# Differential attention in a decoder layer: q, k and v projected in six groups of 512 columns, kept in memory as rows, and read back by half heads

## The chip, the core and the metric

The kernel runs on one core of a Trainium2 chip. TensorE (PE) multiplies; PEld is its load of the stationary operand, which overlaps PE. VectorE (DVE), ScalarE (ACT) and GpSimd (POOL) work beside it, and SyncE (SP) issues nearly all DMAs, one after the other. Each of these engines runs its own instructions in order. The metric is the device time of one execution in microseconds, as the median of several runs.

## The reference, cut to what matters

One layer with three parallel branches, a gated merge and an MLP, on 1024 positions of width 1024, in float32. Only branch B, the differential attention, is touched:

```
proj = rms_norm(x, norm_mix_g) @ w_in              # dq, dk, dv are 1024 columns each
q = rms_norm(dq per head and half, q_g); k = rms_norm(dk per head and half, k_g)
s = q @ k^T * scale, causal                         # 8 heads x 2 halves of width 64
a = softmax(s of half 0) - lam * softmax(s of half 1)
o = rms_norm(a @ v, subln_g) * (1 - lam_init)       # v: 128 columns a head
```

The gates of the merge, `h @ w_gate`, are 3072 further columns of a projection of the same h. Nothing in the attention needs them; the kernel uses them as filler.

## The kernel before, in words

All products are made of float32r pieces: `split` turns a float32 tile into a high part (an ACT cast) and a low part (a DVE subtraction), and `mm3` issues three matmuls for each pair of split operands. The normed input lies in SBUF for the whole stage as `hT` (8 blocks of 128 features, high and low, 1024 positions).

Branch B is `branch_d`. It walks through 64 steps `s`: 8 heads times 8 blocks of 128 query positions. A step computes the scores of both halves (`scores`: PE, then a mask and maximum on DVE, an exponential on ACT), combines them (`combine`, DVE), transposes the result one step later (`turn`: PE into a bank of PSUM, split by ACT and DVE), and two steps later multiplies it with v (`values`). Between these pieces `fill(n)` advances a generator by n units; a unit is the `mm3` of one of the 8 feature blocks, three matmuls. Instructions of PE are pinned: they stay in the order in which the code is written. The other engines' orders are set by a scheduler when the kernel is built, and each engine then keeps to its order.

The generator is `d_gemm`, and gate projections (`gate_steps`) when it has run out. Before the change it works by half heads: for each of 8 heads it loads and splits 8 weight tiles of 384 columns (128 of q, of k and of v), and for each of the head's 8 blocks of positions it fills one PSUM bank in 8 units of 3 matmuls with 384 moving columns. ACT then copies q and k out of the bank (`draw`), squares them and casts v; DVE subtracts v's low part from the bank (`dv`) and sums the squares. After four blocks, half a head is ready: `rsqrt_mean` on POOL, then three late pieces at fixed units of the next half: `q_` (four transposes on PE into `pr`, a split into `dsg`, four DMAs), `s_` (k times its reciprocal norm: four DVE products on `draw`) and `k_` (four transposes, a split, four DMAs to `dk`). The banks of the projection are two, `mm0` and `mm1`, in turn; `pr` takes the one that is not being filled, and the projection's next tile takes the bank of `pr`. So k_'s split has to be done when the next tile begins.

`branch_d` starts with `fill(60)`, then 8 units a step. Of the 12 groups of gate columns (32 units each), the first 6 run before the branch, the last two of these alone on PE, and the rest within it and after it.

Of the kernel before, what the change touches and what calls it, by code (L numbers as in the profile page):

```python
# [10 lines left out]
F32 = mybir.dt.float32  # L11
# [9 lines left out]
NT = 8  # L21
# [50 lines left out]
class Layer:  # L72
# [11 lines left out]
    nmm, kmm = 0, 2  # L84
# [362 lines left out]
    def gate_steps(self, runs):  # L447
# [4 lines left out]
        for run in runs:  # L452
            for r in range(run):
# [3 lines left out]
                for q in range(4):  # L457
# [401 lines left out]
    def d_gemm(self, pool, kv, done):  # L859

        nc = self.nc
        V = nc.vector
        late = []

        def prep(raws, rr, vh):

            qT = pool.tile([P, 2, 512], F32R, tag="dq", name=self.name("dq"))
            kk = pool.tile([P, 2, 2, 512], F32R, tag="dk", name=self.name("dk"))
            rows = [slice(0, 64), slice(64, 128)]

            def turned(j):
                pt = self.other_tile()
                for i in range(4):
                    self.transpose(pt[:, i * P : (i + 1) * P], raws[i][:, j * P : (j + 1) * P])
                return pt, pool.tile([P, 2, 512], F32R, tag="dsg", name=self.name("dsg"))

            def q_():
                pt, sg = turned(0)
                self.split(sg[:, 0], sg[:, 1], pt, self.gd)
                for c in range(2):  # L880
                    for h in range(2):
                        nc.sync.dma_start(f32(qT[rows[h], c]), f32(sg[rows[c], h]))

            def s_():
                for i in range(4):
                    k_ = raws[i][:, P : 2 * P].rearrange("p (c d) -> p c d", c=2)
                    self.pin(V.tensor_mul(k_, k_, rr[:, i, 2:4].unsqueeze(2).broadcast_to([P, 2, 64])))

            def k_():
                pt, sg = turned(1)  # L890
# [4 lines left out]
                kv.append((qT, kk[:, 0], kk[:, 1], vh, rr))  # L895

            return [(4, q_), (5, s_), (13, k_)]
# [3 lines left out]
        def wload(hd, k):  # L901
            r = self.rp.tile([P, 768], F32, tag="raw", name=self.name("raw"))
            nc.sync.dma_start(r.rearrange("p (k n) -> p k n", k=2), self.a["wd"][hd][:, k : k + 2, :])
            raw[hd, k] = r[:, 0:384]
            raw[hd, k + 1] = r[:, 384:768]

        def wsplit(hd, k, w):
            t = self.wp.tile([P, 2, 384], F32R, tag="w", name=self.name("w"))
            self.split(t[:, 0], t[:, 1], raw.pop((hd, k)))
            w[k] = (t[:, 0], t[:, 1])  # L910
            if k == 1:
                wload(hd, 6)

        nw = {}
        for j in range(16):
            hd, hf = divmod(j, 2)
            if j == 0:
                wload(0, 0)
                wload(0, 2)
                wload(0, 4)  # L920
                for k in range(NK):
                    wsplit(0, k, nw)
            if hf == 0:
                w, nw = nw, {}
            rr = pool.tile([P, 4, 4], F32, tag="drr", name=self.name("drr"))
            vh, raws = [], []
            for i in range(4):
                t = hf * 4 + i
                ps = self.mm_tile(384)
                for k in range(NK):  # L930
                    s = slice(t * P, (t + 1) * P)
                    self.mm3(ps, (self.hT[:, k, 0, s], self.hT[:, k, 1, s]), w[k], k == 0, k == NK - 1)
                    if hf and hd < 7:
                        if i == 1 and k == 0:
                            wload(hd + 1, 0)
                            wload(hd + 1, 2)
# [834 lines left out]
```

## Time and profile before

| | |
|---|---|
| median of 3 runs | 2215.06 us (2214.48 to 2216.39) |
| the profiled execution | 2213.57 us, its span 2211.8 us |
| busy in the span | PE 98%, PEld 84%, DVE 62%, ACT 44%, POOL 24% |
| granted clock of TensorE | 0.995 over the span, 1.00 in every stretch read here |
| DMA | 273 MB, mean 123 GB/s |

Branch B with its projections takes from about 620 us to 1150 us. PE busy is the share of time in which at least one matmul was under way; since a matmul's record is longer than the distance to the next one's start, rates are read from starts, not from durations. Where 28 matmuls are shown merged in one row, the next row's start tells when the last of them had gone in.

### The profile page before, as it was taken

Reading aid. Unit: us, or ns where it says so; the run is one execution under the profiler, and the core shown is the slowest. Engines: PE = TensorE matmul, PEld = TensorE weight load, DVE = VectorE, ACT = ScalarE, POOL = GpSimd, SP = SyncE. Lnnn points to the kernel's source line nnn. Section 1 sums busy time; section 2 is a strip of 40 time slices with the busy share of each in tenths; the row PEclk is TensorE's granted clock in tenths of the full one; section 3 lists DMA queues with packets and bytes.
Section 4 is the critical chain, followed back from the end, with each engine's and each line's share of the span. In section 5 each row is a group of like instructions: output and inputs, shape, how many; then the busy total and the mean of one; then the engine's idle time right before and its main releaser. Section 6 shows DMA issues by size and latency. Waiting matters only on the chain.

```text
span 2211.8 us, 30588 instructions
## 1 busy us (share of the span) xinstructions
PE 2163.4 (98%) x11097; PEld 1860.7 (84%) x11097; DVE 1361.4 (62%) x2598; ACT 980.7 (44%) x1962; POOL 527.8 (24%) x696
## 2 busy tenths in 40 slices
PE   7999999999999999999999999999999999899999
PEld 5878888898899999999888888877787888688887
DVE  6643575565237777777641232544688877767779
ACT  6543355454336666666542120223444444543332
POOL 2100000000011111111000003202557655565553
PEclk9999999999999999999999999999999999999999
DMA  7023122121333333333343443436435444854444
GB/s 250 29 81 115 50 91 76 44 82 39 107 109 86 93 84 84 88 92 86 101 148 114 134 142 126 138 110 205 147 115 198 159 147 147 318 196 146 145 145 170
DMA packets 127948, 273.06 MB, mean 123 GB/s; under 512 B 12945, under 2 KB 21430, under 8 KB 125750
## 3 DMA queue, kind: packets, MB, share of 16 engines
q1 hardware_dynamic: 125494, 258.53, 37.2%
q10 hardware_dynamic: 2304, 12.58, 1.4%
q8 instruction: 87, 1.43, 0.3%
q14 instruction: 63, 0.52, 0.1%
HBM read 178.76 MB, written 67.14 MB: 111 GB/s over the span
## 4 chain that ended last, share of the span: by engine, by line
PE 77%; DVE 9%; DMA 6%; ACT 4%; issue 2%; POOL 2%; SPq 0%; DVEq 0%; ACTq 0%; POOLq 0%
PE mm L91 46%; PE p L91 20%; PE sc L91 6%; PE tp L94 2%; PE po L91 2%; DVE acc L67 1%; DMA kraw<-y 1%; DMA xr<-h_d 1%; DVE wo L67 1%; DMA y<-yd 1%; DVE u L67 1%; DVE w L112 1%; DMA wraw<-in_wup 0%; DVE xts L67 0%; DVE c L67 0%
## 5 line engine op out<-in xcount | busy, mean ns | idle before, releaser
L91 PE MATMUL mm<-w,hT 128*128 128x384 f32 (+3 forms) x2496 | 473.4, 332 | 8.3 <-DVE dsg L112 5.4
L91 PE MATMUL mm<-hT,w 128*128 128x512 f32 x1920 | 465.7, 395 | 0.0
L91 PEld LDWEIGHTS mm<-hT,w 128*128 128x128 f32 x1920 | 353.5, 188 | 74.2
L91 PEld LDWEIGHTS mm<-w,hT 128*128 128x128 f32 x2496 | 389.2, 190 | 22.2 <-DVE dsg L112 7.6
L91 PE MATMUL p<-xd,wo 128*128 128x512 f32 x1344 | 310.0, 393 | 5.7 <-DVE c L67 2.2
L91 PE MATMUL p<-xo,wo 128*128 128x512 f32 x1344 | 308.2, 390 | 5.7 <-DVE st L1418 2.6
L91 PEld LDWEIGHTS p<-xd,wo 128*128 128x128 f32 x1344 | 253.8, 189 | 61.7 <-DVE c L67 3.3
L91 PEld LDWEIGHTS p<-xo,wo 128*128 128x128 f32 x1344 | 251.0, 188 | 61.5 <-DVE u L67 3.7
L91 PE MATMUL mm<-kt,w 128*128 128x512 f32 x1152 | 262.2, 389 | 1.9 <-ACT w L111 1.1
L112 DVE TENSOR_TENSOR w<-raw,w 128x256 fp32r<-128x256 f32 (+3 forms) x304 | 173.0, 590 | 137.9 <-ACT w L111 136.8
L91 PEld LDWEIGHTS mm<-kt,w 128*128 128x128 f32 x1152 | 216.0, 188 | 47.9 <-ACT w L111 1.5
L111 ACT CAST w<-raw 128x256 fp32r<-128x256 f32 (+3 forms) x304 | 154.3, 530 | 178.9 <-PE mm L91 114.5
L104 ACT CAST wo<-wraw 128x896 fp32r<-128x896 f32 x122 | 115.0, 945 | 208.9 <-PE p L91 115.2
L67 DVE TENSOR_TENSOR wo<-wraw,wo 128x896 fp32r<-128x896 f32 x122 | 143.7, 1195 | 59.4 <-ACT wo L104 59.4
L1145 POOL TENSOR_TENSOR wraw<-wraw 128x128 f32<-128x128 f32 x128 | 97.3, 760 | 245.8 <-DMA wraw<-in_wdown 108.1
L1007 ACT ACTIVATE dpe<-sc,dst,drr 128x256 f32<-128x256 f32 (+7 forms) x128 | 106.7, 834 | 99.7 <-DVE dst L1003 92.0
L999 DVE CUSTOM_DVE_ANT_0 sc<-sc,tmask 128x256 f32<-128x256 f32 (+7 forms) x128 | 97.0, 758 | 12.6 <-PE sc L91 12.5
L127 POOL TENSOR_SCALAR hss<-hss 128x4 f32<-128x4 f32 x8 | 3.3, 410 | 415.4 <-ACT mscr L752 272.9
L91 PE MATMUL sc<-dk,dq 128*128 128x512 f32 (+3 forms) x384 | 90.4, 343 | 0.0
L1148 POOL TENSOR_TENSOR wraw<-wraw 128x128 f32<-128x128 f32 x128 | 85.6, 669 | 10.0
L1146 POOL TENSOR_TENSOR wraw<-wraw 128x128 f32<-128x128 f32 x128 | 87.3, 682 | 0.0
L1147 POOL TENSOR_TENSOR wraw<-wraw 128x128 f32<-128x128 f32 x128 | 87.2, 682 | 0.0
(283 smaller groups left out, 2832.6 us busy)
## 6 DMA issues: line engine op xcount, KB each, us to landing
dk<-dsg SPq DMA_DIRECT2D x64, 256.0 KB, 4.4
wraw<-in_wup SPq DMA_DIRECT2D x64, 256.0 KB, 3.4
r_d<-xts SPq DMA_DIRECT2D x16, 1024.0 KB, 4.1
wraw<-in_wdown SPq DMA_DIRECT2D x64, 256.0 KB, 3.1
xd<-r_d SPq DMA_DIRECT2D x19, 768.0 KB, 7.4
xd<-r_d SPq DMA_DIRECT2D x14, 1024.0 KB, 6.8
raw<-in_wgate SPq DMA_DIRECT2D x48, 256.0 KB, 3.2
gates<-gt SPq DMA_DIRECT2D x48, 256.0 KB, 2.0
```

What stands on the lines that cost most here:

```text
L67: return self.tc.keep_in_program_order(f(*a, **k))
L91: self.pin(self.nc.tensor.matmul(out, l, r, start=start, stop=stop))
L94: self.pin(self.nc.tensor.transpose(out, x, self.ident))
L104: self.A.copy(hi, src)
L111: nc.scalar.copy(hi, src)
L112: nc.vector.tensor_sub(lo, src, f32(hi))
L999: V.tensor_tensor_reduce(out=sc[:, 0:n], in0=sc[:, 0:n], in1=self.tmask[:, D - n : D], scale=1.0, scalar=-3.0e38, op0=ALU.add, op1=ALU.max ...
L1007: nc.scalar.activation(pe[c][:, 0:n], sc[:, 0:n], AF.Exp, bias=t8[:, 2 + c : 3 + c], scale=rr[:, i, c : c + 1], accum_out=t8[:, 4 + c : 5 ...
L1145: G.tensor_add(r[:, 4], r[:, 0], r[:, 3])
L1146: G.tensor_sub(r[:, 5], r[:, 4], r[:, 1])
L1147: G.tensor_sub(r[:, 6], r[:, 1], r[:, 0])
L1148: G.tensor_sub(r[:, 7], r[:, 2], r[:, 5])
```

## The change

Projections are made in six groups of 512 columns instead of eight of 384 (the columns stay in the order of heads, so a head's 384 columns lie in one group or in two). Each finished tile of 128 positions and 512 columns is copied out of PSUM whole by ACT (`dev`) and stored to a new tensor in memory (`qkv`). A half head is read back from there as four tiles `draw` of 128 x 384, at unit `y` counted from the start; its square sums, `q_`, `s_`, v's split and `k_` follow at fixed distances from `y` (7 to 10, 14, 17 to 20, 16 to 19, 22). k's scaling and the subtraction for v's low part are on GpSimd, which reads SBUF. A half head is read 36 units before the step that starts it would be reached at 24 units a half, the branch begins with `fill(112)`, and a step has 6 units. Five `draw` buffers remain of seven, sixteen for v of seventeen; weight tiles are 10 of 512 columns instead of 13 of 384, raw ones 4 of 512 instead of 3 of 768. One group of gates runs alone before the branch, not two; the branch and what follows it take up the other.

```
@@ class Layer
-    nmm, kmm = 0, 2
+    nmm, kmm, gtight = 0, 2, False
@@ gate_steps
-                        if q >= 2 and k % 2 and (r < run - 1 or self.gnext):
+                        due = q == 2 and k in (2, 5) or q == 3 and k < 6 if self.gtight else q >= 2 and k % 2
+                        if due and (r < run - 1 or self.gnext):
@@ d_gemm
+        def prep(j, y):
+            hd, hf = divmod(j, 2)
+            raws, vh, one = [], [], {}
+            def load(i):
+                r = pool.tile([P, 384], F32, tag="draw", name=self.name("draw"))
+                nc.sync.dma_start(r, self.qkv[hf * 4 + i, :, hd * 384 : (hd + 1) * 384])
+                raws.append(r)
+            def stats(i):
+                if i == 0:
+                    one["rr"] = pool.tile([P, 4, 4], F32, tag="drr", name=self.name("drr"))
+                scr = pool.tile([P, 256], F32, tag="dscr", name=self.name("dscr"))
+                nc.scalar.activation(scr, raws[i][:, 0:256], AF.Square)
+                nc.vector.tensor_reduce(
+                    one["rr"][:, i], scr.rearrange("p (a d) -> p a d", a=4), axis=AX.X, op=ALU.add
+                )
+                if i == 3:
+                    rl = one["rr"].rearrange("p a b -> p (a b)")
+                    self.rsqrt_mean(rl, rl, 64, 16)
...
-            def s_():
-                for i in range(4):
-                    k_ = raws[i][:, P : 2 * P].rearrange("p (c d) -> p c d", c=2)
-                    self.pin(V.tensor_mul(k_, k_, rr[:, i, 2:4].unsqueeze(2).broadcast_to([P, 2, 64])))
+            def s_(i):
+                k_ = raws[i][:, P : 2 * P].rearrange("p (c d) -> p c d", c=2)
+                G.tensor_mul(k_, k_, one["rr"][:, i, 2:4].unsqueeze(2).broadcast_to([P, 2, 64]))
...
+            def v_(i):
+                v = pool.tile([P, 2, P], F32R, tag="dv", name=self.name("dv"))
+                nc.scalar.copy(v[:, 0], raws[i][:, 256:384])
+                G.tensor_sub(v[:, 1], raws[i][:, 256:384], f32(v[:, 0]))
+                vh.append(v)
+            for i in range(4):
+                at(y + i // 2, load, i)
+                at(y + 7 + i, stats, i)
+                at(y + 17 + i, s_, i)
+                at(y + 16 + i, v_, i)
+            at(y + 14, q_)
+            at(y + 22, k_)
+        for j in range(16):
+            prep(j, first + step * j - lead)
...
+        for g in range(6):
+            for t in range(NT):
+                ps = self.mm_tile()
+                s = slice(t * P, (t + 1) * P)
                 for k in range(NK):
                     self.mm3(ps, (self.hT[:, k, 0, s], self.hT[:, k, 1, s]), w[k], k == 0, k == NK - 1)
+                    if g < 5:
+                        if t == 5 and k % 2 == 0:
+                            wload(g + 1, k // 2)
+                        if t == 6 and k in (2, 5) or t == 7 and k < 6:
+                            wsplit(g + 1, len(nw), nw)
+                    elif t == 6 and k in (2, 5) or t == 7 and k < 6:
                         self.gate_load()
+                    y += 1
+                    for f in work.pop(y, []):
+                        f()
                     if k < NK - 1:
+                        yield
+                o = pool.tile([P, 512], F32, tag="dev", name=self.name("dev"))
+                nc.scalar.copy(o, ps)
+                nc.sync.dma_start(self.qkv[t, :, g * 512 : (g + 1) * 512], o)
+                yield
...
@@ branch_d
+        FIRST, LEAD = 112, 36
+        gemm = self.d_gemm(kv, pool, FIRST, 24, LEAD)
+        self.gtight = True
-        fill(60)
+        fill(FIRST)
...
                 scores(s, 0)
-                fill(3)
+                fill(2)
...
-            if s < NS:
-                fill(2)
-            else:
-                fill(6)
+            fill(1 if s < NS else 6)
@@ run
-                    self.gates = self.gate_steps((2, 1, 1, 2, 6))
+                    self.gates = self.gate_steps((2, 1, 1, 1, 7))
```

What the engines' orders become is shown at three places. The first is PE where `k_` transposes k of the fourth half head, in the kernel before: `pr` is the transposed k, `po` the product with v, `sc` a score, `mm` the projection's tile, of which two units are still to come.

```order
L91 MATMUL mm_7231<-w_7058,hT 128x384 x3
L94 MATMUL pr_7267<-ident,draw_6800 128x128
L94 MATMUL pr_7267<-ident,draw_6900 128x128
L94 MATMUL pr_7267<-ident,draw_6998 128x128
L94 MATMUL pr_7267<-ident,draw_7096 128x128
L91 MATMUL po_7279<-dv_6496,daT_7237 128x256
L91 MATMUL po_7279<-dv_6496,daT_7237 128x128
L91 MATMUL mm_7231<-w_7067,hT 128x384 x3
L91 MATMUL mm_7231<-w_7093,hT 128x384 x3
L91 MATMUL sc_7299<-dk_6718,dq_6717 128x384 x2
L91 MATMUL mm_7305<-w_6931,hT 128x384 x3
```

Two units of `mm_7231` are left behind the transposes; then `mm_7305` takes the bank of `pr`. The same transposes in the changed kernel, at a later head; the first row is the last of the four.

```order
L94 MATMUL pr_8697<-ident,draw_8352 128x128
L91 MATMUL mm_8684<-w_8411,hT 128x512 x3
L91 MATMUL sc_8718<-dk_8300,dq_8166 128x384 x2
L91 MATMUL mm_8684<-w_8433,hT 128x512 x3
L91 MATMUL mm_8684<-w_8441,hT 128x512 x3
L91 MATMUL po_8738<-dv_8211,daT_8690 128x256
L91 MATMUL po_8738<-dv_8211,daT_8690 128x128
L91 MATMUL mm_8684<-w_8466,hT 128x512 x3
L91 MATMUL sc_8747<-dk_8300,dq_8166 128x384 x2
L91 MATMUL mm_8684<-w_8483,hT 128x512 x3
L94 MATMUL tp_8756<-ident,dpe_8623 128x128 x2
L91 MATMUL mm_8684<-w_8501,hT 128x512 x3
```

Six units of `mm_8684`, not two, now stand between the transposes and the next tile, which takes the bank of `pr`.

The second place is ACT behind the same transposes, before: `daT` is a cast of the transposed probabilities, `dpe` an exponential, `dsg` the cast of the transposed k.

```order
L111 CAST daT_7237<-tp_7235 128x128
L1007 ACTIVATE dpe_7153,dst_7154<-sc_7225,dst_7154,drr_6432 128x256
L1007 ACTIVATE dpe_7249,dst_7251<-sc_7252,dst_7251,drr_6432 128x384
L111 CAST dsg_7272<-pr_7267 128x512
L1058 ACTIVATE doS_7282<-po_7279,dst_7048 128x128
L947 COPY draw_7291<-mm_7231 128x256
```

And in the changed kernel, where `dscr` is the square of a tile that has been read back, and `dv` v's high part:

```order
L1023 ACTIVATE dpe_8624,dst_8625<-sc_8678,dst_8625,drr_8080 128x256
L111 CAST daT_8690<-tp_8688 128x128
L111 CAST dsg_8702<-pr_8697 128x512
L888 ACTIVATE dscr_8804<-draw_8729 128x256
L919 CAST dv_8924<-draw_8729 128x128
L1023 ACTIVATE dpe_8715,dst_8717<-sc_8718,dst_8717,drr_8080 128x384
L1074 ACTIVATE doS_8741<-po_8738,dst_8524 128x128
L888 ACTIVATE dscr_8816<-draw_8734 128x256
L919 CAST dv_8945<-draw_8734 128x128
L919 CAST dv_8952<-draw_8736 128x128
L111 CAST daT_8759<-tp_8756 128x256
L1023 ACTIVATE dpe_8716,dst_8717<-sc_8747,dst_8717,drr_8080 128x384
```

The cast of k has moved ahead of the exponential of the next step, and two instructions on a tile read back from memory stand ahead of that exponential.

The third place is SP behind the same transposes, in the changed kernel. `qkv_d` is the new tensor.

```order
L972 DMA qkv_d<-dev_8675 128x512
L881 DMA draw_8729<-qkv_d 128x384
L881 DMA draw_8734<-qkv_d 128x384
L881 DMA draw_8736<-qkv_d 128x384
L914 DMA dk_8696<-dsg_8702 64x2x512 x4
L972 DMA qkv_d<-dev_8765 128x512
```

Three of the next half head's four reads stand there, ahead of this half's DMAs to `dk`; they write the buffers that the transposes have just read.

## Rows read from the trace of the kernel before

**Rows 1.** What PE waited for from 640 to 1135 us: total, times, longest
```profile
PE mm L91 <- DVE dsg L112: 5.4, 7, 0.9
PE mm L91 <- DVE dsg L115: 0.5, 1, 0.5
```
**Rows 2.** Two heads: length, busy PE, PEld, DVE, ACT, POOL; clock, DMA share, GB/s
```profile
826.70:885.10 58.40, 57.48 (x374) 55.49 (x373) 45.47 (x133) 36.39 (x93) 8.62 (x8) 1.00 0.38 91
885.10:943.50 58.40, 57.48 (x374) 55.48 (x373) 45.47 (x133) 36.37 (x93) 8.62 (x8) 1.00 0.37 91
```
**Rows 3.** Timeline of PE: start, length, what; 384 and 512 columns between attention pieces
```profile
720.11 1.73 PE L91 MATMUL mm<-w,hT 128*128 128x384 f32 x9
721.68 0.60 PE L94 MATMUL pr<-ident,draw 128*128 128x128 f32 x4
...
1086.84 2.28 PE L91 MATMUL mm<-hT,w 128*128 128x512 f32 x9
1088.95 0.80 PE L91 MATMUL po<-dv,daT 128*128 128x256 f32 x6
...
1103.91 2.21 PE L91 MATMUL mm<-hT,w 128*128 128x512 f32 x9
1105.97 1.26 PE L91 MATMUL po<-dv,daT 128*128 128x256 f32 x10
```
**Rows 4.** Timeline of ACT, gates alone on PE: one tile of 24 matmuls each
```profile
1196.99 0.69 ACT L471 ACTIVATE gt<-mm,dv 128x512 f32<-128x512 f32 x1 [3.04 <-PE mm L91]
1202.43 0.69 ACT L471 ACTIVATE gt<-mm,dv 128x512 f32<-128x512 f32 x1 [4.75 <-PE mm L91]
```
**Rows 5.** Timeline of all engines where PE waits for k_'s split
```profile
722.80 0.67 ACT L1007 ACTIVATE dpe<-sc,dst,drr 128x384 f32<-128x384 f32 x1 [1.54 <-DVE dst L1003]
723.39 0.51 PE L91 MATMUL sc<-dk,dq 128*128 128x384 f32 x2
723.47 0.57 ACT L111 CAST dsg<-pr 128x512 fp32r<-128x512 f32 x1
724.07 0.69 DVE L112 TENSOR_TENSOR dsg<-pr,dsg 128x512 fp32r<-128x512 f32 x1 [0.97 <-ACT dsg L111]
724.82 0.44 PE L91 MATMUL mm<-w,hT 128*128 128x384 f32 x1 [0.91 <-DVE dsg L112]
```
**Rows 6.** Groups by shape, 640 to 1135 us: busy us, mean ns, idle before
```profile
L112 DVE TENSOR_TENSOR w<-raw,w 128x384 fp32r<-128x384 f32 x51 | 27.6, 553 | 0.5
L112 DVE TENSOR_TENSOR dv<-mm,dv 128x128 fp32r<-128x128 f32 x60 | 17.0, 283 | 0.1
L887 DVE TENSOR_TENSOR draw<-draw,drr 128x128 f32<-128x128 f32 x64 | 14.2, 283 | 0.0
L949 ACT ACTIVATE dscr<-mm 128x256 f32<-128x256 f32 x60 | 23.5, 392 | 0.0
L111 ACT CAST dv<-mm 128x128 fp32r<-128x128 f32 x60 | 16.4, 273 | 0.0
```
**Rows 7.** Tile wraw, in the MLP: duration ns min/median/max, first and last start
```profile
L1146 POOL TENSOR_TENSOR wraw<-wraw x128: 451/466/2517, 1416.3 to 2188.7; 128x128 f32<-128x128 f32 x128
L67 DVE TENSOR_TENSOR wo<-wraw,wo x122: 1074/1093/2171, 1588.0 to 2197.7; 128x896 fp32r<-128x896 f32 x122
```
**Rows 8.** DMA issues of the whole run: KB each, median us to landing
```profile
dk<-dsg SPq DMA_DIRECT2D x64, 256.0 KB, 4.4
gates<-gt SPq DMA_DIRECT2D x48, 256.0 KB, 2.0
raw<-in_wd SPq DMA_DIRECT2D x32, 384.0 KB, 3.2
gl<-gates SPq DMA_DIRECT2D x48, 256.0 KB, 2.7
```
**Rows 9.** Tile raw, 560 to 1200 us: landing of all its loads
```profile
DMA to landing us min/median/max: 2.6/3.3/5.8
```
**Rows 10.** Timeline: a combine on DVE, and PE's transposes that read it
```profile
727.98 0.61 DVE L1020 SCALAR_TENSOR_TENSOR dpe<-dpe,dst,dpe 128x384 f32<-128x384 f32 x1
...
731.24 0.49 PE L94 MATMUL tp<-ident,dpe 128*128 128x128 f32 x3
```
**Rows 11.** Timelines of SP and PE ahead of the branch: first load, gates alone
```profile
571.42 0.33 SPq L441 DMA_DIRECT2D raw<-in_wgate  x1
...
575.53 44.40 PE L91 MATMUL mm<-hT,w 128*128 128x512 f32 x192
```

More of the change, by code (lines that the diff above doesn't have):

```diff
@@ L856, in branch_m, with d_gemm, turned @@
         self.pinned = False
[L859 removed]
+    def d_gemm(self, kv, pool, first, step, lead):
         nc = self.nc
[L862 to L872, printed above, removed]
[L873 to L875 removed]
+        G = nc.gpsimd
+        slab, work = [], {}
+        at = lambda y, f, *x: work.setdefault(y, []).append(lambda: f(*x))
+        rows = [slice(0, 64), slice(64, 128)]
+        def turned(raws, c):
+            pt = self.other_tile()
+            for i in range(4):
+                self.transpose(pt[:, i * P : (i + 1) * P], raws[i][:, c * P : (c + 1) * P])
+            return pt, pool.tile([P, 2, 512], F32R, tag="dsg", name=self.name("dsg"))
+        def prep(j, y):
[16 more added lines that the diff above has]
+                    self.rsqrt_mean(rl, rl, 64, 16)
             def q_():
[L878 removed]
+                one["q"] = pool.tile([P, 2, 512], F32R, tag="dq", name=self.name("dq"))
+                pt, sg = turned(raws, 0)
                 self.split(sg[:, 0], sg[:, 1], pt, self.gd)
@@ L907, in wsplit @@
[L907 to L920, printed above, removed]
-                for k in range(NK):
[L922 to L931, printed above, removed]
-                    self.mm3(ps, (self.hT[:, k, 0, s], self.hT[:, k, 1, s]), w[k], k == 0, k == NK - 1)
[L933 to L936, printed above, removed]
-                            wload(hd + 1, 4)
-                        if i >= 2 and k % 2 == 1:
-                            wsplit(hd + 1, i % 2 * 4 + k // 2, nw)
-                    elif hf and i >= 2 and k % 2 == 1:
@@ L941, in d_gemm @@
                         self.gate_load()
-                    while late and late[0][0] <= i * NK + k:
-                        late.pop(0)[1]()
+                    y += 1
+                    for f in work.pop(y, []):
+                        f()
                     if k < NK - 1:
-                        yield True
-                rw = pool.tile([P, 256], F32, tag="draw", name=self.name("draw"))
-                nc.scalar.copy(rw, ps[:, 0:256])
-                scr = pool.tile([P, 256], F32, tag="dscr", name=self.name("dscr"))
@@ L958, in d_gemm @@
-            late = prep(raws, rr, vh)
-            assert j < 4 or done[0] >= (j // 2 - 1) * 8
-        for n in range(NK * 4):
+                        yield
[3 more added lines that the diff above has]
+                yield
+            w, nw = nw, []
+        while True:
             next(self.gates)
-            while late and late[0][0] <= n:
-                late.pop(0)[1]()
-            yield True
+            y += 1
+            for f in work.pop(y, []):
+                f()
+            yield
@@ L1639, in run @@
             self.h2d = dt("h2_d", (8, P, D))
+            self.qkv = dt("qkv_d", (NT, P, 3 * D))
             self.rd = dt("r_d", (16, P, 7, 512))
```

58 lines of the change are left out of this document (27 added, 31 removed).

## The prediction, made before the changed kernel was run

> **What bounds the kernel now.** I first read what PE waited for in branch B. From 640 to 1135 us it waited 5.9 us, all of it for one thing: the low part of `dsg`, the split of transposed q or k, which DVE makes out of the bank that the projection wants next [rows 1]. Then the windows, two heads side by side: both are 58.40 us long, with the same number of instructions. PE is busy 57.48 of that, DVE 45.47, ACT about 36.4, POOL 8.62; the clock is granted in full (1.00 is 2.4 GHz) and the DMA engines are busy 0.38 of the time [rows 2]. So the branch runs at PE's pace, and each head loses about one wait of at most 0.9 us. Two things can move the time: PE's own work, and waits that PE gains or loses. Work taken off DVE is worth nothing by itself.
>
> Records of matmuls overlap, so I take the rate from starts. Nine projection matmuls of 384 columns between two attention pieces take 721.68 - 720.11 = 1.57 us, 174.4 ns each; nine gate matmuls of 512 columns between such pieces take 2.11 and 2.06 us, 234.4 and 228.9 ns, mean 231.7 [rows 3]. Alone on PE, where ACT's evictions come every 5.44 us for 24 matmuls, 512 columns cost 226.7 ns [rows 4].
>
> **The wider groups.** Before: 8 heads x 8 blocks x 8 features x 3 = 1536 matmuls, 1536 x 174.4 ns = 267.9 us. After: 6 x 8 x 8 x 3 = 1152. Of these 112 x 3 = 336 run ahead of the first score and cost 336 x 226.7 = 76.2 us; 816 lie between attention pieces and cost 816 x 231.7 = 189.1 us. Together 265.3: **-2.6 us**. With all at the rate of quiet gates it is 261.2 (-6.7), with all at the slower block 270.0 (+2.1). I take the mixture, as most are interleaved and the block mean is nearest to them. The rest of PE's work stays: the scores, transposes and products with v are as many as before, the pieces into which a step cuts the projection are five before and after, and gates taken from ahead of the branch come back in it and behind it at the same width.
>
> **The wait for k_'s split.** At 722.80 ACT is in an exponential for which it waited 1.54 us on DVE; the cast of k, whose input is ready, stands behind it and starts at 723.47; DVE subtracts at 724.07; PE starts the next tile at 724.82 after 0.91 us idle [rows 5]. What PE did before began at 723.39 and is two matmuls of 384, so it could have gone on at 723.39 + 2 x 0.174 = 723.74: the stop costs 1.08 us where 0.91 is recorded. Scaled, 5.9 us recorded are 5.9 x 1.08 / 0.91 = 7.0. After the change six units stand between the transposes and the tile that takes their bank, not two; six are 18 x 231.7 ns = 4.2 us, and the cast stands ahead of the exponential that had waited for DVE. Transposes, cast and subtraction need about 0.6 + 0.57 + 0.69 = 1.9 us [rows 3, 5], leaving 2 us and more. I take **-7.0 us**, with bounds 0 (another wait of the same length takes its place) and -8.5 (the 8 stops at 1.08 us each).
>
> **What DVE, ACT and GpSimd get.** DVE loses 64 subtractions for v (283 ns) and 64 scalings (283 ns), 36 us in all, 4.5 us a head; its 64 weight subtractions of 553 ns become 48 of about 553 x 512 / 384 = 740, 36 instead of 35 us [rows 6]. PE covers all of it; with that cover gone the 36 us would count in full. ACT's work stays about what it was: squares (392 ns) and v's casts (273 ns) keep their number, and 48 copies of 512 columns, each some 0.57 us as the cast of the same size [rows 5, 6], stand for 64 copies of 256. GpSimd gets 128 operations of 128 x 128. The same shape in the MLP takes 466 ns in the median: 128 x 0.466 = 60 us, 7.5 us a head on an engine that is busy 8.62 of 58.40 [rows 2, 7]. They must fit between the read-back and `k_`: a load (3.2 us), four squares on ACT (about 2 us), rsqrt (8.62 / 2 = 4.3 us a half), four scalings (1.9), about 12 us, with gaps perhaps 15. `k_` stands 21 units behind the reads, and a half of 24 units lasts 58.40 / 2 = 29.2 us, so 25.5 us are there. Cost **0**; were the chain later by 10 us and more, PE would wait at every `k_`.
>
> The row of the MLP has a tail, 2517 ns for a product that else takes 466, and DVE's two-input subtractions there reach 2171 for 1093 [rows 7]. The Trainium skill ("SBUF — State Buffer", section on SBUF's two separate sides) says that a GpSimd operation and a DVE operation with two SBUF inputs lock each other out of a shared port. By that rule DVE would be held 45.5 - 4.5 + 7.5 = 48.5 us of some 57 a head, still less than PE; what it would make of single late pieces is a rival below.
>
> **The rows through memory.** 48 stores of 256 KB and 64 loads of 196 KB add 25 MB in about 450 us, 55 GB/s on top of 91, at a DMA share of 0.38 [rows 2], which would go to about 0.6. Tile stores as large land after 2.0 us, weight loads after 3.2, `gl` loads after 2.7, the head's own `dk` DMAs after 4.4 [rows 8]; single weight loads lie between 2.6 and 5.8 [rows 9]. The closest store to its load is five units away, 5 x 3 x 0.2317 = 3.5 us, and with most of a step's attention in between (58.40 / 8 - 24 x 0.1744 = 3.1 us a step [rows 2, 3]) about 5.9 us: hidden.
>
> New is what stands on ACT. Behind `k_` three reads wait for the transposes to free their buffers, and squares and casts of these tiles stand ahead of the next exponential. The reads land some 3.2 us after the transposes; squares and casts of two tiles, 2 x (0.39 + 0.27), and the exponential, 0.7, end some 5.3 us after them [rows 5, 6, 8], and two dependent DVE operations of about 0.6 us end at 6.5. By the order PE wants the combined rows about 11 units behind the transposes, 11 x 0.695 = 7.6 us and 2.4 us of attention, 10 us. So a load may be late by about 3 us before PE notices. At present a combine ends at 728.59 and its transposes start at 731.24 [rows 10], a slack of 2.65 us. Two kinds of places are tighter: the ends of the groups, where eight weight splits crowd ACT and by the same reckoning about 1 us is left, and the start, where the first `dk` is wanted 14 units behind its `k_`, 14 x 0.68 = 9.5 us, against 1.9 + 4.4 = 6.3 us and whatever SP still has before it. Weights of group 0 are in time: SP's first loads were at 571.42, and the gates alone, 44.40 us for two groups, end half as long after 575.53, at about 598 [rows 11]. I allow **+1.0 us** for all this, from about three waits of 0.3 us; bounds 0 and +16, which is 1.1 us in 15 halves, the price of one stop of the present kind.
>
> **The sum.** -2.6 - 7.0 + 1.0 = -8.6 us. The profiled execution took 2213.57 us, so 2205.0; the median of the runs is 1.5 us above it, so 2206.5 is forecast for the median of 2215.06. What the measurement can tell from no change is about 0.2%, 4.4 us, so "faster" begins below 2210.6.
>
> **Rivals.** *Late reads hold ACT, slower.* The reads of the next half stand at a fixed place in ACT's order, ahead of an exponential. If they land 6 us after the transposes and not 3.2 (the slowest weight load took 5.8, `dk` 4.4 in the median [rows 8, 9], and there is more traffic), combine comes at 9 to 10 us, and each half pays around a microsecond: 15 x 1.1 = 16.5, against the 2.6 of the wider groups and the 7.0: 2215.1 - 2.6 - 7.0 + 16.5 = 2222. It decides from a landing of about 6 us on. For it: two waits in one chain, in-order SP. Against: the medians leave 3 us. Chance 0.12.
>
> *The wait only moves, no change.* PE then waits for another piece as long as before (the bank that `q_` takes, the first `dk` of a half, GpSimd's tail [rows 7] before `k_`), so 0 instead of -7.0, and the wide matmuls give between -2.6 and +2.1: 2212 to 2217. For it: DVE's order is dense, 45 of 58 us, and the present wait too arose from order, not from load. Against: six units of room. Chance 0.22; a further 0.02 that it costs more than the 4.4 us.
>
> *More than forecast.* All wide matmuls go at the quiet rate and no new wait appears: -6.7 - 7.0 = -13.7, 2201.4. The block of 228.9 speaks for it, that of 234.4 against [rows 3]. Chance 0.08.
>
> *GpSimd holds DVE.* Where a subtraction of DVE that PE waits for runs as long as the worst of [rows 7], it is late by a microsecond. If 64 of the 128 operations each put such a piece back by 0.2 us on PE's path, that is 64 x 0.2 = +12.8, with the terms above 2219, slower; below 0.05 us each it is lost in the rest. That 58.40 - 45.47 = 13 us of a head are idle on DVE [rows 2] speaks against it. It has 0.03 of the 0.17 for slower. The page of the Trainium skill named above speaks for such waits.
>
> **How the numbers follow.** The forecast with its own range, 2201 to 2210, has 0.53, and with the case of more it is 0.61 for faster. No change has 0.22, slower 0.17 (late reads 0.12, GpSimd's holds 0.03, the moved wait 0.02). From the case of more (2201) to the edge where late reads or a moved wait cost a few microseconds (2219) leaves out about 0.1 below and 0.1 above.
>
> **What the changed profile would show.** Waits of PE in the branch for `dsg` gone or below 1 us in all, and a head in 56.9 to 57.6 us rather than 58.40: right. Nine matmuls of 512 columns between attention pieces in 2.06 to 2.11 us: the wider groups are sized rightly. ACT idle ahead of `dscr` for a DMA, followed by PE waiting for DVE's `dpe` through `tp`: the late reads. PE waiting at `pr` for POOL's `draw`: the scaling is too slow. DVE busy about 41 us a head, POOL about 16, either way. What would make me wrong is a wait of PE, once a half, for a name that is not in [rows 1].

## The result, and the profile after

The changed kernel takes **2224.81 us** in the median of 5 runs (2222.98 to 2229.44); the kernel before took 2216.39 us beside it (2214.48 to 2219.12). The ratio is 1.0042, with a 95% interval of 1.0027 to 1.0057: 6 to 13 us slower, where 8.6 us less were forecast. The time lies outside the forecast's range of 2201 to 2210 us and above its outer edge of 2219 us. The profiled execution's span is 2225.9 us.

What PE waited for from 640 to 1135 us in the changed kernel (total, times, longest) answers to [rows 1]:

```profile
PE po L91 <- DVE daT L112: 7.2, 14, 1.0
PE pr L94 <- ACT gt L472: 2.1, 3, 0.9
PE sc L91 <- ACT dpe L1023: 1.1, 3, 0.6
PE tp L94 <- DVE doS L1075: 0.7, 2, 0.5
PE tp L94 <- DVE dpe L1036: 0.5, 1, 0.5
```

Both rows of [rows 1] are gone: PE no longer waits for `dsg`. Five others stand in their place, 11.6 us in all, and the largest is the low part of `daT`, the transposed probabilities, ahead of the product with v. The same view of the kernel before has a third row, which [rows 1] leaves out:

```profile
PE po L91 <- DVE daT L112: 0.5, 2, 0.3
```

So PE waited 6.4 us there, not 5.9, and the wait that has grown, from 0.5 to 7.2 us, was already in that trace.

Two heads, from first score to first score, in the columns of [rows 2]:

```profile
789.83:848.80 58.97, 57.79 (x325) 48.90 (x324) 41.03 (x111) 34.86 (x86) 16.73 (x24) 1.00 0.46 125
848.80:908.31 59.51, 58.32 (x325) 48.99 (x324) 42.23 (x115) 35.83 (x87) 16.33 (x24) 1.00 0.50 142
```

In these two DVE has 41 to 42 us of work where it had 45.5, POOL 16.5 where it had 8.6, as the prediction counted. They nevertheless take 59.0 and 59.5 us, not 58.4, at the same granted clock of 1.00 (2.4 GHz), and they are the shortest of the six from the second head to the seventh; the others take up to 60.7 us. The heads are no longer alike, either: where the splits of a group's weights fall differs from head to head.

One of the stops, on PE, ACT and DVE (start, length, what, idle before):

```profile
839.27 0.44 PE L94 MATMUL tp<-ident,dpe 128*128 128x128 f32 x2 [0.19 <-DVE doS L1075]
842.57 1.20 PE L91 MATMUL po<-dv,daT 128*128 128x256 f32 x9
844.12 0.56 PE L91 MATMUL po<-dv,daT 128*128 128x128 f32 x3 [0.35 <-DVE daT L112]
...
840.59 0.42 ACT L888 ACTIVATE dscr<-draw 128x256 f32<-128x256 f32 x1 [0.97 <-DVE drr L889]
840.91 1.08 ACT L1023 ACTIVATE dpe<-sc,dst,drr 128x896 f32<-128x896 f32 x1
842.46 0.38 ACT L111 CAST daT<-tp 128x256 fp32r<-128x256 f32 x1
...
842.12 0.17 DVE L1032 RECIPROCAL dst<-dst 128x2 f32<-128x2 f32 x1 [0.57 <-ACT dpe L1023]
842.58 1.15 DVE L1036 SCALAR_TENSOR_TENSOR dpe<-dpe,dst,dpe 128x896 f32<-128x896 f32 x1
843.64 0.42 DVE L112 TENSOR_TENSOR daT<-tp,daT 128x256 fp32r<-128x256 f32 x1
```

The transposes were started at 839.27 and took 0.44 us. Their cast on ACT starts only at 842.46: ahead of it in ACT's order stands the second exponential of the *next* step, and behind that a copy. The exponential was late in its turn: ACT had stood for 0.97 us before the square of a tile that was read back (`dscr`), until DVE had done a sum of squares (`drr`). DVE's low part stands behind the reciprocal, which waits for that exponential, and behind the combine. So the transposes that PE needs were ready early, and their split stood in two queues. Of the 14 stops for `daT`, 6 have such a wait of `dscr` for DVE in the 6 us before them; in the other 8 an exponential had waited there for its own maximum.

This is the rule in the changed kernel, not the exception. In the traces I counted the steps (63 that have a next one) in which the last cast of `daT` stands behind the second exponential of the next step on ACT: **12 of 63 before, 53 of 63 after**. DVE's order turned with it: the last low part of `daT` stands behind the reciprocal of the next step in 12 of 63 steps before and in 52 of 63 after.

### The profile page after: what moved, and what is told of

Same layout as the page of the kernel before. It is cut to its first block, busy times and chain, and to the rows that moved or that the text cites. A ratio compares the mean times of both kernels' runs of the same rounds, so it can differ in the third digit from the quotient of the medians.

```text
span 2225.9 us, 30073 instructions
## 1 busy us (share of the span) xinstructions
PE 2170.1 (97%) x10713; PEld 1809.4 (81%) x10713; DVE 1342.0 (60%) x2454; ACT 984.4 (44%) x1930; POOL 592.4 (27%) x824
## 4 chain that ended last, share of the span: by engine, by line
PE 71%; DVE 13%; DMA 6%; ACT 5%; issue 3%; POOL 2%; SPq 0%; DVEq 0%; ACTq 0%; POOLq 0%
PE mm L91 42%; PE p L91 21%; PE sc L91 4%; DVE sc L1015 2%; PE tp L94 2%; ACT dpe L1023 2%; PE po L91 2%; DVE acc L67 1%; DVE dpe L1036 1%; DMA xr<-h_d 1%; DVE wo L67 1%; DVE w L112 1%; DMA draw<-qkv_d 1%; DVE u L67 1%; DVE daT L112 1%
## 5 line engine op out<-in xcount | busy, mean ns | idle before, releaser
L91 PE MATMUL mm<-hT,w 128*128 128x512 f32 x1920 | 477.2, 397 | 0.0
L91 PE MATMUL mm<-w,hT 128*128 128x512 f32 (+2 forms) x2112 | 457.6, 360 | 2.5 <-ACT w L111 2.4
L91 PEld LDWEIGHTS mm<-w,hT 128*128 128x128 f32 x2112 | 334.4, 190 | 43.5 <-ACT w L111 3.0
L91 PEld LDWEIGHTS mm<-kt,w 128*128 128x128 f32 x1152 | 216.2, 188 | 45.5 <-DVE w L112 0.7
L1156 POOL TENSOR_TENSOR wraw<-wraw 128x128 f32<-128x128 f32 x128 | 95.5, 746 | 248.3 <-DMA wraw<-in_wdown 124.8
L920 POOL TENSOR_TENSOR dv<-draw,dv 128x128 fp32r<-128x128 f32 x64 | 34.9, 558 | 215.2 <-ACT dv L919 211.2
L1159 POOL TENSOR_TENSOR wraw<-wraw 128x128 f32<-128x128 f32 x128 | 88.6, 692 | 10.0
L91 PEld LDWEIGHTS po<-dv,daT 128*128 128x128 f32 x576 | 76.1, 189 | 18.6 <-DVE daT L112 13.0
```

What stands on the lines that cost most here:

```text
L91: self.pin(self.nc.tensor.matmul(out, l, r, start=start, stop=stop))
L920: G.tensor_sub(v[:, 1], raws[i][:, 256:384], f32(v[:, 0]))
L1156: G.tensor_add(r[:, 4], r[:, 0], r[:, 3])
L1159: G.tensor_sub(r[:, 7], r[:, 2], r[:, 5])
```

## The experiments

Each ran in five rounds beside the kernel before, whose median was 2213.9 to 2214.5 us there. The ratios are to it; "us" made from ratios take 2215 us for it.

**cast_first.** The exponential is issued behind the transposes' casts, and these and DVE's operations around them are pinned in that order:

```
-            nc.scalar.activation(
+            return lambda: self.pin(nc.scalar.activation(
                 pe[c][:, 0:n], sc[:, 0:n], AF.Exp, ...
...
-            self.split(aT[:, 0, ...], aT[:, 1, ...], pt[:, ...])
+            self.pin(nc.scalar.copy(hi, pt[:, 0 : nb * P]))
+            self.pin(V.tensor_sub(lo, pt[:, 0 : nb * P], f32(hi)))
...
-                scores(s, 1)
+                e1 = scores(s, 1)
...
                 turn(s - 1, 1)
             if s < NS:
+                e1()
...
-            V.reciprocal(t8[:, 6:8], t8[:, 4:6])
+            self.pin(V.reciprocal(t8[:, 6:8], t8[:, 4:6]))
```

> The changed kernel with one edit to ACT's and DVE's order: the second exponential of a step is issued behind the casts of the transposed probabilities of the step before (and DVE's low parts of these stand before the reciprocal). Theory of the order (the 7.6 us that PE waits for daT, and much of the short stops around it, come from casts that stand behind an exponential whose maximum is late): waits for daT fall below 2 us, and the kernel takes 2212 to 2217, 8 to 12 less than the changed one. Rival, GpSimd's part of the change: no change, 2222 to 2227. Rival, reads from memory late on ACT: waits for daT stay above 5 us, no change.

Measured: 2210.84 us (2208.27 to 2216.34), ratio 0.9985 (0.9976 to 0.9995). The last cast now stands behind the exponential in 11 of 63 steps, about as before the change, and DVE's low part behind the reciprocal in 6. Against the changed kernel that is 1.0042 - 0.9985 = 0.0057, 12.6 us (roughly 9 to 17 by the two intervals). The largest of PE's waits in the same stretch as above:

```profile
PE pr L94 <- ACT gt L472: 1.9, 3, 0.7
PE po L91 <- DVE daT L1053: 1.8, 2, 1.1
PE tp L94 <- DVE dpe L1036: 1.5, 3, 0.6
```

From the first score to the last product with v, each in its profiled execution, the changed kernel and cast_first:

```profile
676.59:1159.01 482.42, 469.86 (x2606) 393.97 (x2605) 340.59 (x915) 291.32 (x701) 117.26 (x172) 1.00 0.47 134
676.21:1146.45 470.24, 463.94 (x2606) 393.89 (x2605) 339.98 (x915) 294.38 (x701) 119.45 (x173) 1.00 0.49 137
```

The two traces have the same matmuls there in the same order, so their starts can be compared one by one. Of the 12.2 us, 10.3 lie ahead of a product with v (`po`) and 2.0 ahead of a score. The 10.3 are more than the 7.2 us of recorded waits for `daT`: 36 products with v start later by over 0.06 us, where the view of waits lists 14 stops, since the overlap of the matmuls' records hides short ones.

And the piece that was shown above, here:

```profile
835.79 0.44 PE L94 MATMUL tp<-ident,dpe 128*128 128x128 f32 x2 [0.49 <-DVE doS L1077]
837.70 1.55 PE L91 MATMUL mm<-w,hT 128*128 128x512 f32 x6
839.09 1.49 PE L91 MATMUL po<-dv,daT 128*128 128x256 f32 x12
...
837.41 0.39 ACT L1052 CAST daT<-tp 128x256 fp32r<-128x256 f32 x1
837.67 1.13 ACT L1023 ACTIVATE dpe<-sc,dst,drr 128x896 f32<-128x896 f32 x1
```

The cast goes 837.41 - 835.79 = 1.62 us after the transposes began, not 842.46 - 839.27 = 3.19, the exponential after it, and the twelve products run without a gap. The theory of the order holds: these 12.6 us are more than the 9.3 us that the changed kernel had lost against the one before. The edit turns the order of ACT and that of DVE back together; no run separates the two.

**cast_behind.** The reverse, in the kernel before: only ACT is pinned, in the order of the writing, exponential first.

```
-            nc.scalar.activation(
+            self.pin(nc.scalar.activation(
                 pe[c][:, 0:n], sc[:, 0:n], AF.Exp, ...
...
-            self.split(aT[:, 0, ...], aT[:, 1, ...], pt[:, ...])
+            self.pin(nc.scalar.copy(hi, pt[:, 0 : nb * P]))
+            V.tensor_sub(lo, pt[:, 0 : nb * P], f32(hi))
```

> The kernel before with ACT's order alone pinned to that of the writing: the second exponential of a step ahead of the casts of the transposed probabilities, as the changed kernel has it in about half of its steps. Theory of the order: PE gets waits for daT of 4 us or more that the kernel before doesn't have, 5 to 15 us slower, 2220 to 2231. Rivals, GpSimd or the reads alone at fault: within 3 us of the kernel before.

Measured: 2260.97 us (2255.27 to 2261.56), ratio 1.0202 (1.0186 to 1.0217), all 63 steps with the cast behind. DVE's order was not pinned and turned along: its low part stands behind the reciprocal in 57 of 63. The largest of PE's waits, 640 to 1135 us:

```profile
PE po L91 <- DVE daT L1037: 27.1, 21, 2.1
```

It is the same wait as in the changed kernel, in a kernel that has neither wide groups, nor rows in memory, nor products of k and v on GpSimd. The sign was foreseen; the size, 45 us, was three times the most that I expected, and "about half of its steps" was wrong too: it is 53 of 63.

Part of the size is the clock. One of the stops, and the two stretches around and behind it, in the columns of [rows 2]:

```profile
839.15 2.87 PE L91 MATMUL po<-dv,daT 128*128 128x256 f32 x14 [2.08 <-DVE daT L1037]
...
836.20:839.60 3.40, 1.32 (x9) 1.03 (x9) 2.87 (x6) 3.37 (x10) 0.00 (x0) 1.00 0.39 113
839.60:843.00 3.40, 3.40 (x16) 3.40 (x16) 2.09 (x5) 0.37 (x1) 0.00 (x0) 0.50 0.58 169
```

PE had stood for 2.08 us, and right behind that the granted clock is 0.50 (1.2 GHz). Five such stretches lie in the branch of this run, 20.4 us in all, so I estimate up to 10 of the 45 us for them. In the changed kernel and in cast_first the clock stays at 1.00 throughout the branch.

**no_gpsimd.** The changed kernel with k's scaling and v's subtraction on DVE:

```
-                G.tensor_mul(k_, k_, one["rr"]...)
+                self.pin(nc.vector.tensor_mul(k_, k_, one["rr"]...))
...
-                G.tensor_sub(v[:, 1], raws[i][:, 256:384], f32(v[:, 0]))
+                nc.vector.tensor_sub(v[:, 1], raws[i][:, 256:384], f32(v[:, 0]))
```

> The changed kernel with k's scaling and the subtraction for v's low part on DVE again, everything else as changed. Theory of the order: ACT's and DVE's rows around the casts stay the same, so the waits for daT stay at 6 to 9 us and the time at 2222 to 2228, perhaps a little more for DVE's 36 us. Rival, GpSimd's part: waits fall, and the time goes to 2209 to 2216. Rival, late reads: as the theory of the order.

Measured: 2255.22 us (2251.70 to 2257.39), ratio 1.0186 (1.0172 to 1.0200), 32 us more than the changed kernel. So taking k's scaling and v's subtraction off GpSimd does not win the loss back; it costs more, which no theory of mine had said.

**cast_first_no_gpsimd.** The same edit on top of cast_first, to see whether DVE's time or the order around it makes those 32 us.

> The changed kernel with the casts first (as the run cast_first) and k's scaling and v's low part on DVE. If DVE's 36 us count by themselves, as 30 us did in the run without GpSimd: 25 to 35 us more than cast_first, 2236 to 2246. If they cost so much only because DVE stood behind late exponentials: 0 to 10 us more, 2211 to 2221.

Measured: 2243.20 us (2240.76 to 2250.31), ratio 1.0130 (1.0111 to 1.0149), 32 us more than cast_first, again. The work that moved to DVE is 36 us, but DVE is not full; the view of waits and DVE's own timeline show another thing:

```profile
DVE draw L906 <- POOL drr L128: 44.2, 15, 3.3
```

```profile
816.67 0.41 DVE L889 TENSOR_REDUCE drr<-dscr 128x4 f32<-128x256 f32 x1
817.00 0.28 DVE L920 TENSOR_TENSOR dv<-draw,dv 128x128 fp32r<-128x128 f32 x1
817.20 0.42 DVE L1053 TENSOR_TENSOR daT<-tp,daT 128x256 fp32r<-128x256 f32 x1
820.39 0.49 DVE L906 TENSOR_TENSOR draw<-draw,drr 128x128 f32<-128x128 f32 x2 [2.78 <-POOL drr L128]
...
817.46 2.90 POOL L128 TENSOR_TENSOR drr<-drr,mhalf 128x16 f32<-128x16 f32 x1
```

DVE sums the last square of a half head, and with only two instructions between wants the reciprocal root that POOL makes out of it in 2.90 us. It stands for 2.78 us, with masks and low parts behind it that PE wants. So it is in all 16 half heads: 0 to 3 instructions lie between, and DVE stands for 2.0 to 3.3 us. The kernel before also scales k on DVE, but there 12 to 14 instructions lie between (2 in the first half head), and DVE does not stand once. Of the 32 us, some 7 can be the clock, which is at 1.2 GHz for 13.6 us of this branch.

**v_on_dve** and **k_on_dve.** Each of the two moves by itself, on top of cast_first.

> cast_first with only the subtraction for v's low part back on DVE (64 x 0.28 = 18 us of DVE's time). If what made the two runs without GpSimd slow is DVE standing for rsqrt ahead of k's scaling (44 us in 15 times there): within 0 to 5 us of cast_first, 2209 to 2216. If DVE's busy time itself counts: half of the 32 us, 2224 to 2229.

> cast_first with only k's scaling back on DVE (64 x 0.28 = 18 us of DVE's time). If DVE standing for rsqrt makes the loss: DVE waits for POOL drr at draw 40 us in 15 times, 25 to 32 us more than cast_first, 2236 to 2243. If busy time counts: half of that, 2224 to 2229.

Measured: v alone 2210.06 us (2204.57 to 2214.90), ratio 0.9982 (0.9970 to 0.9993), which is cast_first; k alone 2217.44 us (2214.51 to 2221.35), ratio 1.0020 (1.0011 to 1.0028), 8 us more. So busy time on DVE is not what counts: about 18 us more of it cost nothing in the one, and 8 us in the other. But the expectation for k alone was wrong too. With v's subtractions on GpSimd the scalings got other places in DVE's order. In 13 half heads 10 to 39 instructions lie between the sum and the scaling, and DVE does not stand; in 3 there is none, and it stands for 3.3 us. DVE's scalings in k_on_dve, and what ended the idle time before them:

```profile
L906 DVE TENSOR_TENSOR draw<-draw,drr 128x128 f32<-128x128 f32 x64 | 17.5, 283 | 10.0 <-DMA draw<-qkv_d 3.3 <-POOL drr L128 3.3 <-DMA qkv_d<-dev 3.3
```

The view names POOL for one of the three waits and DMAs for the other two, but all three end 3.31 us after the last sum, as in cast_first_no_gpsimd. On PE they show as these:

```profile
PE po L91 <- DVE daT L1053: 4.1, 3, 2.0
PE pr L94 <- DVE draw L906: 3.1, 2, 2.4
```

So DVE stands 16 times where the loss is 32 us (42.4 us in 15 of them in no_gpsimd, within 640 to 1160 us), three times where it is 8 us, and never where there is none. That fits the place of the scaling in DVE's queue as the cause. I did not run the same DVE work with the scalings moved back by hand.

**k_early.** The kernel before with the stop taken away by itself:

```
-            return [(4, q_), (5, s_), (13, k_)]
+            return [(4, q_), (5, s_), (9, k_)]
```

> The kernel before with one number changed: k_ at unit 9 of a half in place of 13, so that six units, not two, stand between its transposes and the tile that takes their bank. If the stop for dsg is worth what the prediction said (7.0 us) and nothing takes its place: PE waits below 1 us in the branch, 2207 to 2210. If the wait only moves: PE waits 4 to 7 us for another name, within 2 us of the kernel before.

Measured: 2212.82 us (2208.91 to 2215.06), ratio 0.9994 (0.9985 to 1.0002). The stop moved, ahead of the transposes instead of behind them:

```profile
PE pr L94 <- DVE dv L112: 5.0, 6, 0.9
```

At unit 9 the other bank, which `pr` wants, has not been read out by v's subtraction.

**k_at_11.** So k_ at unit 11, between the two readers.

> The kernel before with k_ at unit 11 of a half, three units behind the start of the tile (in place of 13; at 9 the stop moved ahead of the transposes, to v's subtraction out of the other bank). If there is room for the transposes between the two banks' readers: PE waits below 1.5 us in the branch, and the kernel takes 5 to 7 us less than before. If DVE's dense order always leaves one of the two late: 3 us or more of waits remain, and the time is within 3 us of before.

Measured: 2209.18 us (2205.51 to 2213.46), ratio 0.9974 (0.9962 to 0.9985), 5.8 us less than before. PE's waits from 640 to 1135 us:

```profile
PE po L91 <- DVE daT L112: 0.5, 2, 0.3
PE mm L91 <- DVE dsg L115: 0.5, 1, 0.5
```

This is the price of the stop: 5.8 us (3 to 8), where the prediction had 7.0. Its heads, without the stop:

```profile
765.85:823.25 57.40, 57.40 (x374) 55.56 (x374) 45.39 (x133) 36.64 (x93) 8.61 (x8) 1.00 0.38 93
```

**no_weight_splits.** cast_first with the first group's weights used for all six groups; the 40 loads and splits of w in the branch are left out, and the first group's columns stand for all.

```
                     if g < 5:
-                        if t == 5 and k % 2 == 0:
-                            wload(g + 1, k // 2)
-                        if t == 6 and k in (2, 5) or t == 7 and k < 6:
-                            wsplit(g + 1, len(nw), nw)
+                        pass
...
-            w, nw = nw, []
```

> The changed kernel with the casts first, and the weights of the first group used for all six: the 40 loads and splits of w inside the branch are left out, so the values are those of other columns. If the stops that are left stem from the bursts of eight splits at the end of a group: every head takes 56.9 to 57.3 us, waits for daT and dpe go to nothing, and the time is 2199 to 2204. Rival, the reads from memory late on ACT, or group boundaries as such: the waits stay, within 2 us of cast_first.

Measured: 2205.78 us (2203.30 to 2207.25), ratio 0.9955 (0.9943 to 0.9968), 6.6 us less than cast_first; a little above the expected range. Two heads next to each other:

```profile
782.91:839.95 57.04, 57.04 (x325) 48.95 (x324) 39.67 (x109) 33.88 (x83) 16.50 (x24) 1.00 0.44 121
839.95:896.98 57.03, 57.03 (x325) 48.97 (x324) 39.66 (x109) 34.02 (x83) 16.20 (x24) 1.00 0.44 121
```

In these PE is busy without a gap. Four of the six heads from the second to the seventh take 57.02 to 57.04 us, instead of 58.40; the other two take 58.06 and 58.77. So the splits account for a good part of the unevenness, not for all.

**squares_later.** cast_first with ACT's squares and casts on the tiles read back kept where they are written:

```
-                nc.scalar.activation(scr, raws[i][:, 0:256], AF.Square)
+                self.pin(nc.scalar.activation(scr, raws[i][:, 0:256], AF.Square))
...
-                nc.scalar.copy(v[:, 0], raws[i][:, 256:384])
+                self.pin(nc.scalar.copy(v[:, 0], raws[i][:, 256:384]))
```

> The changed kernel with the casts first, and the squares and casts of the read-back tiles kept on ACT where they are written, 7 to 10 and 16 to 19 units behind the reads, no longer right behind k_'s cast. Rival of late reads: ACT no longer waits for DMA draw, PE's stops fall, 3 to 6 us less than cast_first. Theory of the order and of the bursts: within 2 us of cast_first (2209 to 2213), as late reads did not reach PE.

Measured: 2212.06 us (2207.24 to 2215.01), ratio 0.9983 (0.9973 to 0.9993): cast_first again. ACT's waits for the reads, which are 20.3 us in cast_first, are gone, and PE gained nothing by it. The test is not clean, though, since a new stop came with it:

```profile
PE pr L94 <- ACT dev L971: 2.9, 1, 2.9
```

The clock falls to 1.2 GHz for 6.8 us at this stop. So a small gain could lie hidden under it.

**splits_apart.** cast_first with the last six splits of a group at every second unit:

```
-                        if t == 6 and k in (2, 5) or t == 7 and k < 6:
+                        if t == 6 and k in (2, 5) or t == 7 and k % 2:
                             wsplit(g + 1, len(nw), nw)
...
+                    if g > 0 and t == 0 and k in (1, 3):
+                        wsplit(g, len(w), w)
```

> cast_first with the last six weight splits of a group at every second unit instead of every unit (the last two in the next group's first tile). If the burst of splits on ACT and DVE makes the stops left in cast_first (5 us in no_weight_splits): half or more of them go, 2206 to 2209. If the number of splits counts and not how close they stand: within 1 us of cast_first.

Measured: 2207.77 us (2207.01 to 2213.85), ratio 0.9972 (0.9963 to 0.9982), 2.9 us less than cast_first. Its PE waits, 640 to 1135 us, sum to 4.1 us, and the largest is

```profile
PE pr L94 <- ACT gt L472: 1.2, 2, 0.7
```

The intervals of the two ratios overlap in part, so the gain is likely, not certain. This version is faster than both kernels, by 0.3% and 0.7%. It is no faster than k_at_11 (0.9974), which changes one number of the kernel before.

**splits_apart_k_later.** A last try on top of it, `q_` at 15 and `k_` at 23 units behind the reads.

> splits_apart with q_ and k_ one unit later (15 and 23 units behind the reads instead of 14 and 22), so that ACT's copy out of the other bank has three units and not two before the transposes want it. If the waits of pr for ACT's gt and dev (2.1 us in cast_first) are this: they go, 1 to 3 us less than splits_apart, 2204 to 2208. Otherwise no change against splits_apart.

Measured: 2210.85 us (2208.17 to 2214.12), ratio 0.9985 (0.9976 to 0.9993). The waits of `pr` went, as expected, but PE then waited 4.0 us in 5 times for the combine (`tp` for DVE `dpe`), and nothing was won. A miss: with the transposes of `q_` and `k_` one unit later, DVE's order differs from splits_apart in 403 of its 2454 places.

## Why the prediction was wrong, step by step

- **What bounds the kernel.** That PE sets the pace was right; that "work taken off DVE is worth nothing by itself" was right only of busy time. v_on_dve shows it: about 18 us more on DVE, no change. But an engine that is idle 13 us a head can still hold PE through what stands first in its queue, and where DVE stood for `drr` in every half head the kernel took 32 us more. The reading of PE's waits was not complete: it was 6.4 us, and not all of it for `dsg`. The 0.5 us for `daT` that were left out are the wait that grew.
- **The wider groups, -2.6.** Borne out as far as it can be read. Six wide matmuls between pieces take 839.09 - 837.70 = 1.39 us in cast_first, 231.7 ns each, the number that the sum used. A head without stops takes 57.03 us in no_weight_splits and 57.40 in k_at_11, 0.4 us less, or 3 us over eight heads. By the sum's own rates it would be 192 x 174.4 - 144 x 231.7 ns, 0.1 us a head; the rest of the -2.6 lies in matmuls ahead of the branch, which no run took by themselves.
- **The wait for k_'s split, -7.0.** The mechanism was right. In the changed kernel the wait is gone, and by itself it is worth 5.8 us (k_at_11), so the term was a little too large. That it may move instead was a rival, and k_early did exactly that.
- **The failed step: new waits, +1.0 with bounds 0 and +16.** The term was made of reads that land late behind `k_`, of a crowd of splits and of the first `dk`, about three waits of 0.3 us. It looked at the wrong place. I had noted that the cast of `dsg` moved ahead of an exponential and took that for a gain; the casts of `daT`, in the same rows of ACT, had moved the other way, behind the exponential, in 53 steps instead of 12, and I did not follow them to PE's product with v. Putting them and DVE's low parts back gives 12.6 us. Added to that are the bursts of eight weight splits at a group's end, where I saw "about 1 us left": 6.6 us with the splits themselves, 2.9 of them likely from how close they stand. So the term was +15.5 us or somewhat more, not +1.0, near its own upper bound. With these the sum closes: -2.6 - 5.8 + 12.6 and 2.9 to 6.6 give +7 to +11 us, and 9.3 were measured. The sign that was named for being wrong came true: PE waits, 14 times in about 15 halves, for a name that is not in [rows 1].
- **The rivals.** *Late reads hold ACT* gave nearly the right time, 2222, which is luck. The reads landed after 3.0 us in the median and 4.5 at most, as the first row below shows, and not 6. ACT did wait for them (the next two rows: in the changed kernel, and in cast_first), but it waits in cast_first as well, where the reads land no earlier (3.4 us in the median, 5.8 at most) and the loss is gone, and none of the 14 stops for `daT` has a wait of ACT for a read in the 6 us before it. *The wait only moves* came nearest: PE waits for another piece. But it is none of the pieces that were named, and the price is higher than "as long as before". *GpSimd holds DVE* is refuted as the cause: cast_first has all of GpSimd's products and none of the loss.
- **GpSimd at cost 0.** It fits in POOL's idle time as counted. What was not seen is that the scaling on DVE would have stood in the new order right behind its sum: with both pieces on DVE that goes with 32 us, with k alone 8 us. A chain of sum, root on POOL and product has to stand somewhere, and on GpSimd nothing queues behind it that PE wants. The kernel before shows that on DVE too it can cost nothing, if enough other work lies between.

The landing of all reads `draw` in the changed kernel, and ACT's waits for them ahead of the squares, 640 to 1135 us:

```profile
DMA to landing us min/median/max: 2.3/3.0/4.5
...
ACT dscr L888 <- DMA draw<-qkv_d: 16.5, 13, 3.1
ACT dscr L888 <- DMA draw<-qkv_d: 13.0, 16, 1.7
```

Left open: why the order of ACT and DVE changed, and how the loss divides between the two. The order is set when the kernel is built; the step now has one wide unit of 3 x 231.7 = 695 ns, not 3 x 174.4 = 523 ns, between the second score and the next transposes, so an exponential may look ready first. That is a guess. no_gpsimd has the same 53 of 63, so it is not GpSimd's part. No run changed the width of a unit alone.

## What to carry to other kernels

When a change alters the length of the pieces between which a scheduler interleaves, compare on every helper engine which of two instructions comes first around each hand-over to the bound engine, and count it over all steps: here the 12 against 53 of 63 could have been counted in the orders before any run, and were worth more than all terms of the sum. A queue that is half idle is no cover if its first instruction waits: a dependent chain across two engines (sum, root, scale) belongs on the engine behind which nothing urgent queues, or needs other work between its links. And a stop for a bank of PSUM has two sides, the reader of the bank that is taken and the reader of the bank that is left; moving the work by two units solved it in one kernel, by four only turned it round. Last, leave no row of a view of waits out because it is small: the small one was the one that grew.

## What the runs showed of the hardware that was not expected

GpSimd's products beside a busy DVE (tile `draw` in the changed kernel, minimum, median and maximum in ns):

```profile
L906 POOL TENSOR_TENSOR draw<-draw,drr x60: 395/402/1249, 675.7 to 1085.3; 128x128 f32<-128x128 f32 x60
L920 POOL TENSOR_TENSOR dv<-draw,dv x59: 451/462/1246, 670.3 to 1077.6; 128x128 fp32r<-128x128 f32 x59
```

DVE's subtractions of 128 x 512, for w with both inputs in SBUF and for `daT` with one in PSUM (busy us, mean ns, idle before):

```profile
L112 DVE TENSOR_TENSOR w<-raw,w 128x512 fp32r<-128x512 f32 x37 | 26.3, 720 | 6.3 <-ACT w L111 6.2
L112 DVE TENSOR_TENSOR daT<-tp,daT 128x512 fp32r<-128x512 f32 x44 | 29.5, 684 | 0.3 <-ACT daT L111 0.3
```

And w's subtraction in no_gpsimd, where GpSimd has no such product:

```profile
L112 DVE TENSOR_TENSOR w<-raw,w 128x512 fp32r<-128x512 f32 x37 | 25.0, 686 | 6.6 <-ACT w L111 6.6
```

Most of GpSimd's products run at the time of the MLP's row [rows 7] or below, some take 1.25 us. Of all 128, 17 took over 520 ns, and during each of these DVE ran an operation with both inputs in SBUF, a subtraction for w or a combine; 96 ran beside none, and none of those took so long. On DVE the subtraction with both inputs in SBUF takes 36 ns more in the mean, 37 x 0.036 = 1.3 us in all, and 2 ns more without GpSimd's products. The rule of the Trainium skill that was weighed in the prediction ("SBUF — State Buffer", section on SBUF's two separate sides) agrees with these tails in kind; on PE's time nothing of it was seen.

The clock inside the branch fell to 1.2 GHz in five of the runs: five times in cast_behind, four in cast_first_no_gpsimd, twice in no_gpsimd, once each in squares_later and k_on_dve. Each time PE had just stood, or was standing, for 1.0 to 2.9 us. In all other kernels it stayed at 1.00 there, the longest single stop that these had from 640 to 1135 us being 1.4 us. So a stop can cost more than its length. Which stops the clock follows, no run here was made to tell.
